# A two-layer transformer kernel: the loads of the modulation weights move from SyncE's queue to GpSimd's

## The chip, the cores and the metric

The kernel runs on one core of one Trainium2 chip. The time is the device time of one execution in microseconds (us): the median of three runs. An engine executes its own instruction list in order; an instruction whose inputs or whose target buffer are not there yet holds everything behind it on the same engine. A DMA is started by an instruction in such a list: SyncE (SP) computes nothing here and only starts DMAs, GpSimd (POOL) computes and starts DMAs.

## The reference

One call computes two blocks on a sequence of 512 tokens with 1024 features, in float32. Block one normalises `x`, projects it with `w_in`, runs a sparse attention of eight heads (compressed, selected and windowed keys) and a stick-breaking attention of eight heads, mixes both and adds an MLP. Block two runs an mLSTM and a block-sparse attention and then a mixture of 32 experts. Both blocks are modulated: a vector `mod = silu(c) @ ada_w + ada_b` of 6 x 1024 numbers is cut into shift, scale and gate for the first half of a block (columns 0, 1, 2) and for its second half (3, 4, 5), and used as

```
u = rms_norm(h, norm1_g) * (1 + scale1) + shift1
h = h + gate1 * mixed
u2 = rms_norm(h, norm2_g) * (1 + scale2) + shift2
h = h + gate2 * ff
```

The second block does the same with `c_2` and `w_ada_2`. Each of the two modulation matrices is 1024 x 6144 float32, 24 MB.

## The kernel before, in words

All large products are made on TensorE (PE) at about float32 accuracy: each weight piece is split by ScalarE (ACT) and VectorE (DVE) into two parts (`parts`, line 118), and three matmuls (`mm3`, lines 128 to 130) take the place of one. A weight piece of 1 MB is loaded by `load` (line 97) on SP's queue into one of two buffers named `raw`; a load waits until the splits of the piece before last are done.

The first two columns of the first modulation matrix are needed at once and are made on TensorE (`ada_first`, line 359, tile `araw` with 12 buffers). The other ten columns are made in the background by `ada` (line 388), off TensorE: for a column r, sixteen loads (line 399) of 128 x 512 float32, 256 KB each, go to a ring of three buffers, also named `araw`; each is multiplied by one number per row and added up. For an even k DVE does it (lines 408 and 410), for an odd k ACT multiplies in place (line 404) and POOL adds (line 406). At the end POOL adds the two sums (line 414), and TensorE adds over the partitions. Columns 2, 3, 4 of the first matrix are made during the attentions and the merge, column 5 and all six of the second matrix during the MLP. That makes 10 x 16 = 160 loads.

The instruction lists are made when the program is built. The code yields the background work in steps (`step`) after each piece of a projection; a planner then simulates the run, and puts on each engine the ready instruction that is earliest in the program, so that work of a later line may stand early in an engine's list where that engine would have been free. `self.order(a, b)` tells the planner to put a behind b: the background's multiplications are put behind the matmul of their step (`self.behind`), and the first loads of column 2 behind `self.first_loads`, the last load of `ada_first`. On the chip the lists then run in that fixed order, whatever the real durations are.

POOL's list in this part of the program also holds: copies for the attention heads (line 506), part of the softmax scaling (line 722), the second half of the split in the stick-breaking heads (line 767), stores and loads of 256 KB of the gates (lines 1094 and 985), part of the norms (lines 185 and 228), and the first weights of the compression (`compress_start`, whose last load is kept as `self.compress_loads`).

Of the kernel before, what the change touches and what calls it, by code (L numbers as in the profile page):

```python
# [72 lines left out]
class Kernel:  # L73
# [314 lines left out]
    def ada(self, which, rounds, together=False):  # L388


        nc = self.nc
        w, bname, c, mods = ((self.a["ada_w"], "ada_b", self.sc[:, 0:8], self.mods),
                             (self.a["w_ada_2"], "b_ada_2", self.sc[:, 8:16], self.mods2))[which]
        for r in rounds:
            acc = [self.apool.tile([128, 1024], F32, name=f"acc{i}", bufs=1) for i in range(2)]
            for k in range(8):
                for at in (0, 512):
                    raw = self.apool.tile([128, 512], F32, name="araw", bufs=3)
                    ins = nc.sync.dma_start(raw, w[0, k * 128:(k + 1) * 128, r * 1024 + at:r * 1024 + at + 512])
                    if which == 0 and r == 2:  # L400
                        self.order(ins, self.first_loads)
                    x = acc[k % 2][:, at:at + 512]
                    if k % 2:
                        ins = nc.scalar.activation(x if k == 1 else raw, raw, AF.Copy, scale=c[:, k:k + 1])  # L404
                        if k > 1:
                            nc.gpsimd.tensor_add(x, x, raw)  # L406
                    elif k == 0:
                        ins = nc.vector.tensor_scalar(x, raw, c[:, 0:1], None, op0=OP.mult)
                    else:
                        ins = nc.vector.scalar_tensor_tensor(x, raw, c[:, k:k + 1], x, op0=OP.mult, op1=OP.add)  # L410
                    self.order(ins, self.behind)
                if k < 7:
                    yield
            self.order(nc.gpsimd.tensor_add(acc[0], acc[0], acc[1]), self.behind)
            if together:
                if r == 0:
                    pick = self.free[:, 2048:2059]
                    nc.vector.tensor_scalar(pick, self.one[:, 0:1].to_broadcast([128, 11]), 0.0, None, op0=OP.mult)
                    nc.vector.tensor_copy(pick[:, 5:6], self.one[:, 0:1])
                    rows = self.ps("O", 1), self.ps("T", 2)  # L420
                parts = [self.free[:, i:i + 1024] for i in (0, 1024)]
                self.order(nc.scalar.activation(parts[0], acc[0], AF.Copy), self.behind)
                nc.gpsimd.tensor_sub(parts[1], acc[0], parts[0])
                for i in range(2):
                    for x in range(2):
                        nc.tensor.matmul(rows[i][:6], pick[:, 5 - r:11 - r], parts[x][:, i * 512:i * 512 + 512],
                                         start=(r + x == 0), stop=(r + x == 6), skip_group_check=True)
                yield
                continue
            ps = self.ps("T", 2)  # L430
            for j in range(8):
                nc.tensor.matmul(ps[:, 2 * j:2 * j + 2], acc[0][:, j * 128:(j + 1) * 128], self.one[:, 0:2],
                                 start=True, stop=True, skip_group_check=True)
            nc.vector.tensor_add(mods[:, r * 8:(r + 1) * 8], ps[:, :16].rearrange("p (j x) -> p j x", x=2)[:, :, 0],
                                 self.col(bname)[:, r * 8:(r + 1) * 8])
            yield
        if together:
            x = self.apool.tile([128, 1024], F32, name="acc1", bufs=1)
            for i in range(2):
                nc.scalar.activation(x[:6, i * 512:i * 512 + 512], rows[i][:6], AF.Copy)  # L440
            ps = self.ps("T", 2)
            for j in range(8):
                nc.tensor.transpose(ps[:, 6 * j:6 * j + 6], x[:6, j * 128:(j + 1) * 128], self.ident[:6, :6])
            nc.vector.tensor_add(mods.rearrange("p (r j) -> p r j", r=6),
                                 ps[:, :48].rearrange("p (j r) -> p r j", j=8),
                                 self.col(bname).rearrange("p (r j) -> p r j", r=6))
            yield
# [1659 lines left out]
```

## Time and profile before

| | |
|---|---|
| median of 3 runs | 1790.49 us (1790.27 to 1791.97) |
| profiled execution | 1795.8 us, of which the span from first to last instruction is 1794.0 us |
| TensorE (PE) busy | 1722.5 us, 96% of the span |
| VectorE (DVE) busy | 1385.7 us, 77% |
| ScalarE (ACT) busy | 1149.6 us, 64% |
| GpSimd (POOL) busy | 461.2 us, 26% |
| mean granted TensorE clock | 0.988 of full speed |
| issues of `araw` on SP, line 399 | 64 of `ada_w` and 96 of `w_ada_2`, 256 KB each, from 27.4 to 824.3 us |

The page gives shares over the whole span, and the change bears on the stretch from 27 to 830 us alone. In a row of waits, "A <- B" reads: instructions of A stood idle until B ended; a bracket such as "[2.29 <-DVE kT L171]" at the end of a row of the timeline is the idle time of that engine just before the row, and what ended it.

### The profile page before, as it was taken

To read this page: it belongs to the slowest core of one execution; us is meant where nothing else is said; L and a number is where in the kernel's file an instruction comes from. 1 tells how busy PE (TensorE), PEld (TensorE's weight loads), DVE (VectorE), ACT (ScalarE), POOL (GpSimd) and SP (SyncE) were. 2 spreads that over 40 slices of the span, in tenths; PEclk is the share of its full clock that TensorE was granted. 3 is DMA by queue.
4 is the path that set the end of the run, shared out by engine and by line. 5 is a ranking of instruction groups with operands and counts; after the bars stand their busy time and mean duration, and the time that the engine had idled before them with its cause. 6 is when DMAs were issued, how large, how long until landed. Compare 5 with 4: busy or idle time off the path is not lost. (4 is left out here: it accounts for less than half of the span.)

```text
span 1794.0 us, 24961 instructions
## 1 busy us (share of the span) xinstructions
PE 1722.5 (96%) x8996; PEld 1414.4 (79%) x8996; DVE 1385.7 (77%) x2028; ACT 1149.6 (64%) x1814; POOL 461.2 (26%) x428
## 2 busy tenths in 40 slices
PE   6999999998999999999999999979999989999996
PEld 3878977887898888888978888757877767787874
DVE  4758788887687474747756877879999979999997
ACT  4646765764555343435555765568888868888886
POOL 2114326435032333333313300111212112121113
PEclk9999999998999999999999999989999999999998
DMA  9543204217446655554432224669999999999954
GB/s 344 172 130 106 78 30 160 87 60 245 149 152 210 201 184 192 187 188 159 141 95 71 71 67 165 233 203 366 366 360 366 327 323 381 374 367 365 371 209 168
DMA packets 234912, 377.71 MB, mean 211 GB/s; under 512 B 11817, under 2 KB 102565, under 8 KB 234784
## 3 DMA queue, kind: packets, MB, share of 16 engines
q1 hardware_dynamic: 223904, 348.22, 56.5%
q0 software_dynamic: 10880, 27.85, 5.2%
q8 instruction: 72, 1.18, 0.3%
q14 instruction: 56, 0.46, 0.1%
HBM read 366.64 MB, written 20.73 MB: 216 GB/s over the span
## 5 line engine op out<-in xcount | busy, mean ns | idle before, releaser
L118 ACT ACTIVATE w<-raw 128x1024 fp32r<-128x1024 f32 (+2 forms) x350 | 353.8, 1017 | 298.4 <-PE G L129 230.5
L118 DVE TENSOR_TENSOR w<-raw,w 128x1024 fp32r<-128x1024 f32 (+2 forms) x350 | 421.9, 1225 | 115.6 <-ACT w L118 113.8
L128 PE MATMUL G<-u,w 128*128 128x512 f32 (+1 forms) x688 | 265.5, 387 | 3.2 <-DVE mo L1090 1.3
L129 PE MATMUL G<-u,w 128*128 128x512 f32 (+1 forms) x688 | 264.4, 385 | 2.0 <-DVE u L922 1.1
L130 PE MATMUL G<-u,w 128*128 128x512 f32 (+1 forms) x688 | 264.7, 386 | 0.6 <-DVE w L118 0.6
L129 PE MATMUL S<-w,x 128*128 128x512 f32 x504 | 200.9, 399 | 0.8 <-DVE w L118 0.8
L128 PE MATMUL S<-w,x 128*128 128x512 f32 x504 | 196.2, 395 | 5.4 <-PEq L1933 5.2
L130 PE MATMUL S<-w,x 128*128 128x512 f32 x504 | 198.2, 393 | 0.0
L118 DVE TENSOR_TENSOR w<-rawa,w 128x1024 fp32r<-128x1024 f32 x122 | 151.2, 1271 | 15.4 <-ACT w L118 15.3
L128 PEld LDWEIGHTS G<-u,w 128*128 128x128 f32 x688 | 129.8, 189 | 30.4 <-issue 2.8
L129 PEld LDWEIGHTS G<-u,w 128*128 128x128 f32 x688 | 129.8, 189 | 27.9 <-DVE u L922 1.6
L118 ACT ACTIVATE w<-rawa 128x1024 fp32r<-128x1024 f32 x122 | 127.7, 1059 | 36.7 <-PE S L130 23.0
L130 PEld LDWEIGHTS G<-u,w 128*128 128x128 f32 x688 | 129.9, 189 | 26.3 <-DVE w L118 1.8
L406 POOL TENSOR_TENSOR acc<-acc,araw 128x512 f32<-128x512 f32 x60 | 87.6, 1479 | 236.8 <-ACT araw L404 236.6
L128 PEld LDWEIGHTS S<-w,x 128*128 128x128 f32 x504 | 95.7, 190 | 27.2 <-issue 5.7
L129 PE MATMUL G<-hid,w 128*128 128x512 f32 (+1 forms) x320 | 111.1, 347 | 1.2 <-DVE hid L1131 1.2
L129 PEld LDWEIGHTS S<-w,x 128*128 128x128 f32 x504 | 95.7, 190 | 20.3 <-DVE w L118 1.1
L130 PE MATMUL G<-hid,w 128*128 128x512 f32 (+1 forms) x320 | 111.3, 348 | 0.0
L130 PEld LDWEIGHTS S<-w,x 128*128 128x128 f32 x504 | 95.7, 190 | 19.7 <-DVE x L1773 0.3
L128 PE MATMUL G<-hid,w 128*128 128x512 f32 (+1 forms) x320 | 110.8, 347 | 0.0
L129 PE MATMUL G<-w,hh 128*128 128x512 f32 x248 | 100.7, 406 | 2.3 <-DVE w L118 0.9
L1737 POOL TENSOR_TENSOR x<-xg,x 128x512 fp32r<-128x512 f32 x30 | 44.9, 1498 | 218.9 <-ACT x L1736 218.9
(652 smaller groups left out, 4028.8 us busy)
## 6 DMA issues: line engine op xcount, KB each, us to landing
raw<-in_mlp_w_dram SPq DMA_DIRECT2D x36, 1024.0 KB, 5.5
raw<-in_w_in_dram SPq DMA_DIRECT2D x33, 1024.0 KB, 5.4
raw<-in_w_expert_up_dram SPq DMA_DIRECT2D x28, 1024.0 KB, 9.6
raw<-in_w_expert_gate_dram SPq DMA_DIRECT2D x27, 1024.0 KB, 9.2
raw<-in_w_expert_down_dram SPq DMA_DIRECT2D x27, 1024.0 KB, 8.1
araw<-in_w_ada_dram SPq DMA_DIRECT2D x96, 256.0 KB, 3.7
rawa<-in_w_expert_gate_dram SPq DMA_DIRECT2D x21, 1024.0 KB, 9.5
rawa<-in_w_expert_up_dram SPq DMA_DIRECT2D x20, 1024.0 KB, 8.5
```

What stands on the lines that cost most here:

```text
L118: ins = nc.scalar.activation(r[0], v, AF.Copy), nc.vector.tensor_sub(r[1], v, r[0])
L128: first = nc.tensor.matmul(ps, lhs[0], rhs[0], start=start, stop=False)
L129: nc.tensor.matmul(ps, lhs[0], rhs[1], start=False, stop=False)
L130: self.behind = nc.tensor.matmul(ps, lhs[1], rhs[0], start=False, stop=stop)
L406: nc.gpsimd.tensor_add(x, x, raw)
L1737: nc.gpsimd.tensor_sub(x[1][:, s], y[:, s], x[0][:, s])
```

## The change

The instruction that starts the 160 loads of `ada` is issued by GpSimd in place of SyncE. The first loads of column 2 are ordered behind the last load of `compress_start`, which is on GpSimd's queue, and no longer behind the last load of `ada_first`, which is on SyncE's. The ring of three buffers, the sizes, the consumers and their order behind the matmuls are the same.

```diff
@@ -396,9 +396,9 @@
             for k in range(8):
                 for at in (0, 512):
                     raw = self.apool.tile([128, 512], F32, name="araw", bufs=3)
-                    ins = nc.sync.dma_start(raw, w[0, k * 128:(k + 1) * 128, r * 1024 + at:r * 1024 + at + 512])
+                    ins = nc.gpsimd.dma_start(raw, w[0, k * 128:(k + 1) * 128, r * 1024 + at:r * 1024 + at + 512])
                     if which == 0 and r == 2:
-                        self.order(ins, self.first_loads)
+                        self.order(ins, self.compress_loads)
                     x = acc[k % 2][:, at:at + 512]
                     if k % 2:
                         ins = nc.scalar.activation(x if k == 1 else raw, raw, AF.Copy, scale=c[:, k:k + 1])
```

## Rows read from the trace of the kernel before

**Rows 1.** Busy time by stretch: length, then each engine's, PEclk, DMA share, GB/s.
```profile
100.00:200.00 100.00, 99.84 (x568) 83.96 (x567) 78.55 (x198) 65.17 (x144) 30.54 (x41) 1.00 0.37 114
280.00:320.00 40.00, 37.25 (x181) 29.44 (x180) 35.51 (x38) 23.12 (x41) 26.27 (x19) 0.99 0.53 171
405.00:440.00 35.00, 30.26 (x119) 23.36 (x119) 24.09 (x39) 18.02 (x30) 19.17 (x25) 0.85 0.72 230
540.00:820.00 280.00, 280.00 (x1255) 230.41 (x1254) 171.06 (x187) 124.76 (x169) 87.34 (x51) 1.00 0.59 192
```

**Rows 2.** Waits from 400 to 445 us: total us, times, longest.
```profile
DVE acc L410 <- DMA araw<-in_ada_w_dram: 7.0, 4, 3.1
ACT araw L404 <- DMA araw<-in_ada_w_dram: 4.5, 3, 3.8
```

**Rows 3.** TensorE's timeline, the longest of five idle times from 412 to 430 us.
```profile
427.76 0.79 PE L129 MATMUL G<-kT,w 128*128 128x512 f32 x1 [2.29 <-DVE kT L171]
```

**Rows 4.** VectorE's timeline in the same stretch: start us, us, work, idle before.
```profile
413.64 1.02 DVE L410 SCALAR_TENSOR_TENSOR acc<-araw,sc,acc 128x512 f32<-128x512 f32 x1 [3.09 <-DMA araw<-in_ada_w_dram]
414.58 0.62 DVE L783 CAST P<-e 128x512 fp32r<-128x512 f32 x2
...
426.35 0.75 DVE L410 SCALAR_TENSOR_TENSOR acc<-araw,sc,acc 128x512 f32<-128x512 f32 x1 [2.49 <-DMA araw<-in_ada_w_dram]
427.02 0.69 DVE L171 TENSOR_TENSOR kT<-sq,qT 128x512 fp32r<-128x512 f32 x1
```

**Rows 5.** Busy time in the two stretches behind the longest idle times.
```profile
417.20:420.40 3.20, 3.16 (x8) 2.51 (x9) 1.94 (x3) 0.18 (x1) 0.00 (x0) 0.50 0.64 243
...
427.70:434.20 6.50, 6.44 (x15) 4.64 (x16) 5.19 (x9) 3.95 (x7) 2.98 (x6) 0.50 0.64 197
```

**Rows 6.** Line 399 by stretch (from 563; 275 to 317; 405 to 440): ns min/median/max, starts.
```profile
L399 SPq DMA_DIRECT2D araw<-in_w_ada_dram x96: 327/328/1147, 563.6 to 824.3; - x96
...
L399 SPq DMA_DIRECT2D araw<-in_ada_w_dram x16: 327/328/383, 275.2 to 316.0; - x16
...
L399 SPq DMA_DIRECT2D araw<-in_ada_w_dram x14: 327/360/588, 406.3 to 438.6; - x14
```

**Rows 7.** A held weight load: its issue on SP, and the split that freed its buffer.
```profile
578.57 0.39 SPq L97 DMA_DIRECT2D raw<-in_mlp_w_dram  x1
...
575.80 1.22 DVE L118 TENSOR_TENSOR w<-raw,w 128x1024 fp32r<-128x1024 f32 x1
```

**Rows 8.** The start: SP's timeline, then the stretch by engine.
```profile
27.37 3.04 SPq L399 DMA_DIRECT2D araw<-in_ada_w_dram  x3
...
20.00:40.00 20.00, 17.64 (x141) 8.64 (x140) 9.21 (x17) 8.20 (x12) 1.93 (x3) 1.00 1.05 383
```

**Rows 9.** ScalarE's waits from 540 to 840 us.
```profile
ACT w L118 <- PE G L129: 138.7, 47, 4.4
ACT acc L404 <- DMA araw<-in_w_ada_dram: 20.4, 8, 6.0
```

**Rows 10.** Issues of loads of 256 KB on POOL, line 985, and their landing.
```profile
L985 POOL DMA_DIRECT2D sg<-md x13: 539/544/573, 414.8 to 451.9; - x13
...
DMA to landing us min/median/max: 3.2/6.2/7.2
```

**Rows 11.** Line 767 on POOL: durations, and who waited for it in the run.
```profile
L767 POOL TENSOR_TENSOR s<-e,s x24: 726/1376/2252, 299.3 to 405.0; 128x512 fp32r<-128x512 f32 x16, 128x256 fp32r<-128x256 f32 x8
...
PE S L770: 0.2, 1
```

**Rows 12.** POOL's timeline: a split, loads of the gates.
```profile
391.39 0.73 POOL L767 TENSOR_TENSOR s<-e,s 128x256 fp32r<-128x256 f32 x1 [4.29 <-DVE s L766]
...
414.85 1.09 POOL L985 DMA_DIRECT2D sg<-md  x2 [0.75 <-DMA md<-mo]
...
431.21 0.56 POOL L985 DMA_DIRECT2D sg<-md  x1 [6.17 <-DVE sg L992]
```

**Rows 13.** SP's longest wait for a buffer from 400 to 445 us, ending at 406.30.
```profile
SPq L399 <- DVE acc L408: 22.7, 1, 22.7
```

## The prediction

> **What bounds the kernel now.** I began with the page: TensorE is busy for 96% of the span, so a change off TensorE can win only where TensorE stands idle, and lose only where it makes TensorE wait. The busy time by stretch says where that is while the background loads run [rows 1]. From 540 to 820 us, where most of them lie, TensorE is busy 280.00 of 280.00 us; from 100 to 200 us it is 99.84 of 100. Two stretches have gaps: 280 to 320 us (2.75 idle) and 405 to 440 us (35.00 - 30.26 = 4.74 idle, granted clock 0.85).
>
> Then I asked who waits for whom in the second of these. VectorE waited 7.0 us and ScalarE 4.5 us for the loads in question [rows 2]. The reader should see in the timelines how this reaches TensorE: an addition of the background (line 410) stands in VectorE's list ahead of a cast and of a split that TensorE needs; it waits 3.09 and 2.49 us for its load [rows 4], and TensorE is idle until the cast, and until the split [rows 3]. Both times the granted clock then is 0.50, which is 1.2 GHz in place of 2.4, for 3.20 and 6.50 us [rows 5]. Half of 9.70 us, 4.85 us, is lost to that. So late loads cost this stretch up to 4.74 + 4.85 = 9.6 us, and the question is whether GpSimd brings them sooner.
>
> **The change part by part.** *What SP gets back.* 160 issues at 0.328 us are 52.5 us of SP [rows 6]. SP computes nothing, so this counts only where a weight load stood behind one of them. The widest case that I found: the split that frees the buffer ends at 577.02, the weight load is issued at 578.57, 1.55 us late [rows 7]; the TensorE of that stretch has no gap. I take 0; a gain of 1.5 us is the other end.
>
> A page's rule can stand beside that. The rows above show issue time that nobody waited for. The Trainium skill, "DMA: Bandwidth & Descriptors", section "Issuing engines are not separate DMA queues", says that starting DMAs from several engines saves only the sequencer's time to start them. This case's rows agree so far as the 52.5 us go; by the rule the change can win no bandwidth.
>
> *The start.* The three first loads leave SP at 27.37 us and would go out behind GpSimd's compression loads instead. They are 0.77 MB, at 383 GB/s 2.0 us of transfer, in a crowded stretch [rows 8]. They stand behind the loads that TensorE waits for there, so moving them frees nothing that is late: 0, and at best -2.0.
>
> *What GpSimd takes on.* A load of the same size takes 0.539 to 0.573 us of GpSimd [rows 10], so 160 of them take about 88 us, and each needs a place in its list. That makes the trip through the ring of three buffers longer: the release of a buffer, the issue, the landing, the use. The issue grows by 0.55 - 0.33 = 0.22 us, and the issue may have to stand behind an instruction of GpSimd.
>
> *The MLP, 540 to 820 us.* 96 loads and most of column 5. GpSimd is busy 87 of 280 us, and 53 to 59 more fit. ScalarE stands 138.7 us waiting for TensorE, and has already swallowed a wait for such a load of 6.0 us without a gap on TensorE [rows 1, 9]. The cover is TensorE's own queue of ready work; it would be gone if a load came more than about 6 us later than now. I take 0; the bad end is one such wait, +6. The stretch from 100 to 200 us has the same cover: 0, bad end +2.75, the gap that 280 to 320 shows.
>
> *The stick-breaking heads, 275 to 317 us.* 16 loads [rows 6], 16 x 0.55 = 8.8 us more on GpSimd, which is busy 26.27 of 40 us there [rows 1]: 35 of 40. Its other work here is the split of line 767, median 1.376 us, for which TensorE waited 0.2 us in all [rows 11]. 16 loads through 3 buffers are 5.3 trips; in 66% of the cases GpSimd is busy when the buffer comes free, and half an instruction is 0.7 us, so a trip is 0.22 + 0.66 x 0.7 = 0.68 us longer and the round 3.6 us. What share reaches TensorE I take from 405 to 440 us: 4.74 idle for 11.5 us waited [rows 1, 2], 41%. That is +1.5 us. Ends: 0 (all hidden) and +8.8 (all of GpSimd's new work on the path).
>
> *The merge, 405 to 440 us.* 14 loads, 4.7 trips [rows 6]; GpSimd is busy 19.17 of 35 us, 55% [rows 1], so a trip is 0.22 + 0.55 x 0.7 = 0.6 us longer, 2.8 us together, of which 41% are 1.1 us of idle time; the clock took as much again as the idle time there (4.85 to 4.74): +2.3 us. There is also a new neighbour: on GpSimd the loads share the list with loads of the gates, one of which held the list 6.17 us until 431.21 [rows 12]. The buffer that line 410 frees at 427.10 [rows 4] would be refilled 4.1 us later if its load stood behind that one; 41% of it is 1.7, with the clock 3.4; I give this even odds, +1.7. Ends of the stretch: -9.6 (both waits gone) and +9.6 (as much again).
>
> Sum: 0 + 0 + 0 + 1.5 + 2.3 + 1.7 = +5.5 us. The profiled execution takes 1795.8 us, 5.3 above the median of 1790.49, and would take 1801.3; against the median that is 1796.0 us.
>
> **The rivals.** *Hidden anyway.* Almost nobody waits for GpSimd today: 0.2 us of TensorE's for line 767 [rows 11], and the 0.22 us per trip could vanish in the covers named. For it: full TensorE in most of the stretch. Against it: the two stretches without cover. Time: 1790.5, give or take 3.
>
> *Faster: the two waits fall out of the order.* The planner places the background's additions where it expects their loads. If, with the loads on another engine, it puts the additions of line 410 behind the cast and the split that TensorE needs, VectorE's two waits hurt nobody, and the 9.6 us come back: 1780.9, and with one of the two, about 1785. It decides at a single place: whether line 410 stands ahead of line 783 and line 171 [rows 4]. For it: the waits show that today's order rests on loads expected sooner than they come. Against it: on GpSimd they come later still, and the planner may go wrong elsewhere.
>
> *Much slower: a load that blocks GpSimd.* SP could afford to wait 22.7 us for a buffer until 406.30 [rows 13]. On GpSimd such a wait holds what follows. Were it placed ahead of the split at 391.39 [rows 12], that would come 14.9 us late: up to 1805.4. Against it: the planner sees both on one engine and would place the load after the split.
>
> *Slower by the port.* VectorE and GpSimd might get in each other's way. But the casts at 414.58, beside two loads issued by GpSimd at 414.85, took 0.62 for two, and the thirteen issues of line 985 never took over 0.573 us [rows 4, 10, 12]. So issuing does not seem to suffer. If it did, with each of the 10 trips 0.88 us longer (the difference of line 767's longest and median [rows 11]), 41% of it with the clock would be about 7 us: 1803. The Trainium skill, "SBUF — State Buffer", the box "The DVE blocks DMA trap (SWDGE)", states that mechanism: while VectorE runs in a two-port mode GpSimd cannot write its descriptors. It gives about 0.62 us alone and 3.1 us beside a copy; by that each trip would be an estimated 2.5 us longer, and the kernel some 20 us slower. The thirteen rows don't bear it out.
>
> **How the numbers follow.** The forecast (+2 to +10) 0.38; hidden 0.25; faster 0.26; blocked 0.07; port 0.04. A change within 0.2%, 3.6 us, can't be told from none here. Nearly all of the forecast's chance and the last two are slower by more than that: 0.47, the rest of the forecast (0.02) going to the same, 0.27; faster 0.26. The forecast's own range is 1792 to 1801. To leave out no more than 2 in 10 the range has to reach to the faster case's full price and past the blocked one's: 1781 to 1807.
>
> **What would show it.** Right: line 399 on POOL's queue at about 0.55 us each; TensorE still full from 540 to 820; in the merge and the stick-breaking heads more waits for `araw` on VectorE and ScalarE than 11.5 us, more idle TensorE, and a clock of 0.50 behind it. Wrong: no wait of line 410 ahead of a cast (the faster case), TensorE's idle time as before (hidden), or a new gap outside the two stretches, above all one that is ended by GpSimd.

## The result, and the profile after

The changed kernel takes 1804.61 us (median of four runs, 1801.05 to 1810.33), the kernel before 1791.23: a ratio of 1.0076, 95% interval 1.0055 to 1.0098, so slower by 13.4 us. A second measurement, beside the experiments, gave 1801.81 us and 1.0055 (1.0040 to 1.0071), 10.7 us. The forecast was slower by 5.5 us.

The program falls into five parts, whose ends can be read from the lines that begin and end them: line 706 is the last product of the sparse attention's heads, line 1128 the first result of the MLP, line 1230 the end of its half of the block, line 2011 the last store, which GpSimd issues. First the kernel before, then the changed one (a row holds count, duration in ns as min/median/max, and the first and last start in us).

```profile
L706 PE MATMUL O<-C,vsc x16: 587/640/692, 150.2 to 267.4; 32*128 32x512 f32 x16
...
L1128 ACT ACTIVATE r<-G x30: 572/578/599, 540.7 to 833.1; 128x512 f32<-128x512 f32 x30
...
L1230 DVE SCALAR_TENSOR_TENSOR h<-G,mods,h x16: 743/748/752, 1091.1 to 1154.9; 128x512 f32<-128x512 f32 x16
...
L2103 POOLq DRAIN  x3: 50/115/5038, 1788.2 to 1793.8; - x3
```

```profile
L706 PE MATMUL O<-C,vsc x16: 587/640/692, 151.2 to 272.0; 32*128 32x512 f32 x16
...
L1128 ACT ACTIVATE r<-G x30: 576/578/601, 544.4 to 845.4; 128x512 f32<-128x512 f32 x30
...
L1230 DVE SCALAR_TENSOR_TENSOR h<-G,mods,h x16: 743/749/752, 1103.4 to 1167.2; 128x512 f32<-128x512 f32 x16
...
L2103 POOLq DRAIN  x3: 50/262/8312, 1799.0 to 1808.3; - x3
```

The attention's end is 4.6 us later (272.0 to 267.4). From there to the MLP's start nothing is lost: 272.4 us after, 273.3 before. The MLP, from the first line 1128 to the last line 1230, takes 622.8 in place of 614.2, so 8.6 more. The experts behind it gain 1.5 in this pair of profiles. The rest is behind the last instruction: GpSimd's closing DRAIN takes 8.312 in place of 5.038 us, and from the start of line 2011 to the end of the span it is 9.4 us in place of 5.6.

The stretches of [rows 1] again, in the changed kernel (length, busy time of PE, PEld, DVE, ACT, POOL, then PEclk, DMA share, GB/s):

```profile
100.00:200.00 100.00, 98.68 (x545) 82.74 (x544) 79.66 (x191) 61.26 (x134) 40.69 (x57) 0.98 0.36 111
280.00:320.00 40.00, 39.06 (x186) 32.02 (x187) 36.02 (x42) 23.93 (x43) 30.30 (x32) 0.96 0.53 171
405.00:440.00 35.00, 31.25 (x142) 24.95 (x141) 29.46 (x47) 18.92 (x34) 22.99 (x33) 0.90 0.58 185
540.00:820.00 280.00, 275.53 (x1232) 227.16 (x1231) 165.60 (x179) 119.80 (x161) 136.03 (x152) 0.98 0.58 186
```

The two stretches that were full have gaps now (1.32 us from 100 to 200, 4.47 from 540 to 820), and the two that had gaps are a little fuller. VectorE's 7.0 us of waits for the loads in the merge [rows 2] have shrunk to this one row:

```profile
DVE acc L410 <- DMA araw<-in_ada_w_dram: 1.1, 1, 1.1
```

The 160 loads are on GpSimd, and their issues cost what [rows 10] said (0.539 us the shortest, 0.539 and 0.547 the medians); landing takes 3.3 us in the median:

```profile
L399 POOL DMA_DIRECT2D araw<-in_w_ada_dram x96: 539/539/582, 572.0 to 836.8; - x96
L399 POOL DMA_DIRECT2D araw<-in_ada_w_dram x64: 539/547/754, 43.1 to 568.1; - x64
...
DMA to landing us min/median/max: 2.8/3.3/9.5
```

**The gap at 580 us.** TensorE's timeline shows two idle times (the bracket at the end of a row is the idle time before it and what ended it):

```profile
578.77 0.39 PE L130 MATMUL G<-hid,w 128*128 128x512 f32 x1
581.88 3.57 PE L432 MATMUL T<-one,acc 128*128 128x2 f32 x16 [2.72 <-POOL acc L414]
587.20 0.80 PE L128 MATMUL G<-hid,w 128*128 128x512 f32 x1 [1.75 <-DVE h L1135]
```

Line 432 is the sum over the partitions that finishes column 5, the gate of the MLP. Without it the first `add` (line 1135) of the MLP's second product can't run, and that product has only two PSUM banks (`G`): when both are full, TensorE has to wait for the gate. GpSimd's timeline shows how its last addition came late, VectorE's what stood between line 432 and the `add`:

```profile
568.11 0.54 POOL L399 DMA_DIRECT2D araw<-in_ada_w_dram  x1 [1.03 <-DVE acc L410]
...
577.25 1.29 POOL L406 TENSOR_TENSOR acc<-acc,araw 128x512 f32<-128x512 f32 x1 [3.42 <-ACT araw L404]
578.49 0.56 POOL L399 DMA_DIRECT2D araw<-in_w_ada_dram  x1
579.06 2.76 POOL L414 TENSOR_TENSOR acc<-acc,acc 128x1024 f32<-128x1024 f32 x1
```

```profile
580.06 2.85 DVE L118 TENSOR_TENSOR w<-raw,w 128x1024 fp32r<-128x1024 f32 x1 [0.43 <-ACT w L118]
585.49 0.17 DVE L434 TENSOR_TENSOR mods<-T,cols 128x8 f32<-128x8 f32 x1 [2.58 <-PE T L432]
585.60 0.88 DVE L408 TENSOR_SCALAR acc<-araw,sc 128x512 f32<-128x512 f32 x2
586.40 1.40 DVE L1135 SCALAR_TENSOR_TENSOR h<-G,mods,h 128x512 f32<-128x512 f32 x2
```

After the gap the granted clock is 1.2 GHz for some ten microseconds (PEclk, third from the end, 0.51):

```profile
582.00:592.00 10.00, 8.25 (x28) 7.16 (x29) 4.59 (x8) 1.44 (x2) 3.02 (x6) 0.51 0.61 200
```

So 4.47 us of idle time and some 4 us by the clock (half of the 8.25 us of work in these ten) make the 8.6. In the profile of the second measurement (a1 below) line 432 waited 0.64 us in place of 2.72, and the MLP took 619.8, 5.6 more than before:

```profile
578.45 1.95 PE L432 MATMUL T<-one,acc 128*128 128x2 f32 x16 [0.64 <-POOL acc L414]
...
582.21 0.80 PE L128 MATMUL G<-hid,w 128*128 128x512 f32 x1 [1.81 <-DVE h L1135]
```

In the kernel before, line 432 came without a wait and ahead of the point where TensorE runs dry, and the `add` came 34.4 us after the MLP's start (575.1 - 540.7) in place of 42.0:

```profile
572.39 1.84 PE L432 MATMUL T<-one,acc 128*128 128x2 f32 x16
...
574.26 0.17 DVE L434 TENSOR_TENSOR mods<-T,cols 128x8 f32<-128x8 f32 x1 [1.99 <-PE T L432]
...
575.14 0.75 DVE L1135 SCALAR_TENSOR_TENSOR h<-G,mods,h 128x512 f32<-128x512 f32 x1
```

**The gap at 170 us.** GpSimd, VectorE and TensorE in the changed kernel:

```profile
163.23 0.55 POOL L399 DMA_DIRECT2D araw<-in_ada_w_dram  x1
163.79 2.40 POOL L414 TENSOR_TENSOR acc<-acc,acc 128x1024 f32<-128x1024 f32 x1
166.13 0.55 POOL L399 DMA_DIRECT2D araw<-in_ada_w_dram  x1
166.69 1.91 POOL L722 TENSOR_TENSOR P<-P,st 128x128 f32<-128x128 f32 x3
```

```profile
163.56 2.67 DVE L711 TENSOR_TENSOR st<-st,gates 128x4 f32<-128x4 f32 x1
...
166.92 2.77 DVE L118 TENSOR_TENSOR w<-raw,w 128x1024 fp32r<-128x1024 f32 x1
```

```profile
170.09 1.06 PE L667 MATMUL S<-kdc,QS 128*128 128x32 f32 x8 [1.32 <-DVE st L696]
```

Line 711, four numbers per partition, takes 0.17 us elsewhere and here 2.67: it ends at 166.23, when GpSimd's addition (line 414) ends. The split of line 118 takes 1.23 us elsewhere and 2.77 beside line 722. The two together hold VectorE for 4 us, and TensorE runs dry behind them. In the kernel before the same addition holds VectorE too, but there it meets a split alone (3.45 us in place of 1.23), and TensorE loses 0.16 us in all from 100 to 200 us [rows 1]:

```profile
166.87 2.38 POOL L414 TENSOR_TENSOR acc<-acc,acc 128x1024 f32<-128x1024 f32 x1
...
166.90 3.45 DVE L118 TENSOR_TENSOR w<-raw,w 128x1024 fp32r<-128x1024 f32 x1
```

The gap is not the whole price. Behind it the granted clock falls: over these 30 us it is 0.94 in the changed kernel, about 1.8 us lost. In the kernel a2 of the experiments the same gap stands, and the clock stays at 1.00 (the changed kernel first, then a2):

```profile
150.00:180.00 30.00, 28.68 (x178) 25.27 (x177) 26.19 (x69) 17.22 (x45) 14.64 (x18) 0.94 0.30 88
...
150.00:180.00 30.00, 28.68 (x183) 24.66 (x184) 26.30 (x68) 17.52 (x45) 14.97 (x20) 1.00 0.27 85
```

### The profile page after: what moved, and what is told of

Its sections match the earlier page's. It is cut to its first block, busy times and chain, and to the rows that moved or that the text cites. A ratio compares the mean times of both kernels' runs of the same rounds, so it can differ in the third digit from the quotient of the medians.

```text
span 1808.6 us, 24940 instructions
## 1 busy us (share of the span) xinstructions
PE 1728.0 (96%) x8996; PEld 1418.7 (78%) x8996; DVE 1397.5 (77%) x2028; ACT 1149.7 (64%) x1814; POOL 545.6 (30%) x588
## 5 line engine op out<-in xcount | busy, mean ns | idle before, releaser
L118 DVE TENSOR_TENSOR w<-raw,w 128x1024 fp32r<-128x1024 f32 (+2 forms) x350 | 431.2, 1251 | 112.3 <-ACT w L118 109.6
## 6 DMA issues: line engine op xcount, KB each, us to landing
raw<-in_w_expert_up_dram SPq DMA_DIRECT2D x28, 1024.0 KB, 11.5
```

Of the source, the lines that this page charges most:

```text
L118: ins = nc.scalar.activation(r[0], v, AF.Copy), nc.vector.tensor_sub(r[1], v, r[0])
```

## The experiments

Every kernel was profiled once and timed. The table gives the parts by the lines named above, in us: the last start of line 706; from there to the first line 1128; from there to the last line 1230; from there to line 2011; from there to the end of the span.

| kernel | loads on GpSimd | to 706 | to 1128 | to 1230 | to 2011 | end | median | ratio to before (95%) |
|---|---|---|---|---|---|---|---|---|
| before | 0 | 267.4 | 273.3 | 614.2 | 633.5 | 5.6 | | |
| changed | 160 | 272.0 | 272.4 | 622.8 | 632.0 | 9.4 | 1804.61 | 1.0076 (1.0055, 1.0098) |
| changed, again | 160 | 271.7 | 271.3 | 619.8 | 630.3 | 9.4 | 1801.81 | 1.0055 (1.0040, 1.0071) |
| e1 second matrix | 96 | 267.7 | 270.4 | 614.0 | 631.3 | 5.4 | 1790.12 | 0.9997 (0.9988, 1.0006) |
| e2 columns 2 to 4 | 48 | 271.3 | 271.4 | 613.6 | 631.7 | 7.9 | 1797.18 | 1.0034 (1.0021, 1.0046) |
| e3 column 5 | 16 | 267.8 | 273.3 | 618.9 | 630.6 | 6.0 | 1799.66 | 1.0052 (1.0039, 1.0066) |
| e4 all but column 5 | 144 | 272.0 | 270.0 | 613.9 | 629.7 | 7.6 | 1797.59 | 1.0040 (1.0026, 1.0054) |
| e6 order alone | 0 | 267.4 | 271.1 | 614.2 | 629.1 | 5.6 | 1790.06 | 0.9994 (0.9984, 1.0004) |
| e8 64 of the second | 64 | 267.1 | 272.0 | 613.9 | 629.8 | 8.5 | 1793.98 | 1.0021 (1.0010, 1.0031) |
| h1 mix | 96 | 266.9 | 272.6 | 613.9 | 629.7 | 5.4 | 1792.45 | 1.0010 (1.0001, 1.0019) |
| a2 gate taken from column 2 | 160 | 269.4 | 271.6 | 614.1 | | | | |
| a3 line 414 on VectorE | 160 | 268.3 | 275.0 | 618.3 | 631.0 | 9.4 | 1804.86 | 1.0082 (1.0065, 1.0098) |
| a4 line 406 of column 5 on VectorE | 160 | 271.2 | 271.8 | 619.3 | 632.1 | 9.3 | 1801.58 | 1.0055 (1.0040, 1.0071) |
| a5 four PSUM banks | 160 | 271.9 | 269.8 | 613.6 | 630.9 | 9.3 | 1798.12 | 1.0035 (1.0023, 1.0048) |

The columns "to 1128" and "to 2011" scatter by some 1.5 us between kernels whose lists are the same there (e1 and before differ by nothing ahead of the MLP, and by 2.9 us in "to 1128"), so single differences of that size mean nothing. The first and the third column fall into two groups each, with 3.4 and 4.1 us between them (a2 and a3 apart in the first); the fifth goes from 5.4 to 9.4.

### Which loads cost

Theory A was that column 5's deadline makes the MLP's 8.6 us and column 2 the attention's; rival B that each load costs its share.

```diff
-                    ins = nc.sync.dma_start(raw, w[0, k * 128:(k + 1) * 128, r * 1024 + at:r * 1024 + at + 512])
+                    ins = (nc.gpsimd if which == 1 else nc.sync).dma_start(raw, w[0, k * 128:(k + 1) * 128, r * 1024 + at:r * 1024 + at + 512])
+                    ins = (nc.gpsimd if which == 0 and r < 5 else nc.sync).dma_start(raw, w[0, k * 128:(k + 1) * 128, r * 1024 + at:r * 1024 + at + 512])
+                    ins = (nc.gpsimd if which == 0 and r == 5 else nc.sync).dma_start(raw, w[0, k * 128:(k + 1) * 128, r * 1024 + at:r * 1024 + at + 512])
+                    ins = (nc.gpsimd if not (which == 0 and r == 5) else nc.sync).dma_start(raw, w[0, k * 128:(k + 1) * 128, r * 1024 + at:r * 1024 + at + 512])
```

(Against the kernel before; the lines added are those of e1, e2, e3 and e4. e2 and e4 take the new order of the first loads too.)

> Only the 96 loads of the second matrix go to GpSimd; those of columns 2 to 5 stay on SyncE. Theory A (column 5's deadline at the start of the MLP costs 8.6 us of it, the attention stage some 4): TensorE has no gap from 605 to 840 us in either trace, so these 96 loads cost nothing: 1791, within 1.5 us, apart from the wait at the very end of the program. Rival B (each load that GpSimd issues costs about the same, 13.4 us over 160): 96/160 of it, 8.0 us, 1799. Rival C (what grows is GpSimd's drain behind the last instruction, with the number of its DMAs): the drain of 5.0 us before, 8.3 us after, should be about 7 here, +2.

> Only the 48 loads of columns 2, 3 and 4 go to GpSimd, with the new order of the first loads. Theory A: the attention stage alone pays, TensorE's last line 706 about 4.6 us later than before (267.4), the MLP begins about 3.7 us later (540.7 before), and column 5, on SyncE, is in time for the first addition of its gate (575.1 before): 1794 to 1796. Rival B (equal cost per load): 48/160 of 13.4, 4.0 us, 1795; told from A by the milestones, which under B would go on falling behind past 540 us. Rival C (drain): about 6 us of drain.

> Only the 16 loads of column 5 go to GpSimd. Theory A: the MLP begins when it did before (540.7 us), but the column is finished late, behind 581 us, TensorE stands at line 432 for the last addition of GpSimd (line 414) and then runs at a granted clock of 0.50: some +8 us, 1798 to 1800. Rival B (equal cost per load): 16/160 of 13.4, 1.3 us, 1792.5.

> All loads but the 16 of column 5 go to GpSimd. Theory A: the change without the wait at line 432: only the 4 us of the attention stage and what the drain takes: 1794 to 1797. Rival B (equal cost per load): 144/160 of 13.4, 12 us, 1803. Rival D (the gap at the MLP's start comes from the change of the instruction lists in all, not from column 5's loads being on GpSimd): a gap of some 8 us of TensorE between 560 and 600 us here too, 1802.

Measured: e1 changes nothing, with 60% of the loads; e3 costs 9.2 us, with 10% of them. Rival B is out. The first column splits the kernels by who issues column 2 (266.9 to 267.8 on SyncE, 271.2 to 272.0 on GpSimd, a3 apart, and a2, whose 269.4 has the gap without the lower clock), the third by who issues column 5 (613.6 to 614.2, against 618.3 to 622.8, a2 and a5 apart). Rival D is out by e4, whose lists are rearranged too, and which has no gap (TensorE is busy for 40.00 of the 40 us from 560 to 600). e2 and e4 came out 1.2 and 0.6 us above the upper ends of theory A's times, in which the drain had no full share. e3's time is in theory A's range, but the gap has another shape than theory A said, and than in the changed kernel:

```profile
575.99 1.95 PE L432 MATMUL T<-one,acc 128*128 128x2 f32 x16
...
580.75 0.80 PE L128 MATMUL G<-hid,w 128*128 128x512 f32 x1 [2.81 <-DVE h L1135]
```

Line 432 does not wait, it is over before 581 us, and the gap still comes. That it is late data alone was thereby in doubt.

### Why column 5 costs

In a2, a4 and a5 (in this order) the changed kernel is altered:

```diff
-                    nc.vector.scalar_tensor_tensor(x, ps, mods[:, 40 + k:41 + k], x, op0=OP.mult, op1=OP.add)
+                    nc.vector.scalar_tensor_tensor(x, ps, mods[:, 16 + k:17 + k], x, op0=OP.mult, op1=OP.add)
-                            nc.gpsimd.tensor_add(x, x, raw)
+                            (nc.vector if which == 0 and r == 5 else nc.gpsimd).tensor_add(x, x, raw)
-                    self.project(hid, "mlp_w2", 0, D, add, f * 8)
+                    self.project(hid, "mlp_w2", 0, D, add, f * 8, banks=() if f else (("G", 2), ("G", 2), ("S", 3), ("S", 3)))
```

> The changed kernel, but the MLP's result is multiplied by column 2 in place of column 5, so that column 5 is made and loaded by GpSimd as before but nothing in the MLP waits for it. Theory A (the deadline): the gap of TensorE at 580 us is gone, and the time is that of the kernel that left column 5 on SyncE, 1797, within 1.5. Rival D (the loads slow the MLP's start in another way, by the DMA engines or by GpSimd's list): the gap stays, 1803 to 1805.

With the deadline gone the MLP takes 614.1 us, and TensorE has no idle row from 540 to 605 us, though column 5 is loaded by GpSimd and finished at 582.1. The times behind line 1230 can't be compared, nor the total (1941.83 us), against what I had expected: with the other gate the numbers that the experts get are others, and behind line 1230 TensorE has 2937 matmuls in place of 2760. That the tokens go to other experts is the likely reason; no run shows it.

> The changed kernel, with the six additions of column 5 that GpSimd makes (line 406) on VectorE, so that GpSimd's list holds loads and the last addition alone there. Theory I (column 5 is late because loads and additions stand in each other's way in GpSimd's list): the column is done before the first addition of its gate, no gap of TensorE at 580 us, 614 us from the MLP's first line 1128 to the last line 1230 in place of 620 to 623: 1796 to 1798. Rival J (each load simply takes longer from GpSimd): still late, 618 to 620, 1800 to 1802.

Theory I fell. The column's data are indeed ready earlier: GpSimd's last addition ends at 575.12, 32.1 us after the MLP's start, in place of 37.4 in the changed kernel (581.82 - 544.4). It doesn't help:

```profile
572.73 2.39 POOL L414 TENSOR_TENSOR acc<-acc,acc 128x1024 f32<-128x1024 f32 x1 [4.66 <-DVE acc L406]
```

```profile
577.67 1.84 PE L432 MATMUL T<-one,acc 128*128 128x2 f32 x16
582.49 0.80 PE L128 MATMUL G<-hid,w 128*128 128x512 f32 x1 [2.98 <-DVE h L1135]
```

Line 432 could have run at 575.1 and runs at 577.67, with no wait: it is where it stands in TensorE's list. Counted in the lists as built, the second product's matmuls ahead of line 432 are 35 in the kernel before, 41 in e4, and 48 in e3, a4 and the changed kernel; two banks take 2 x 24 = 48. So with column 5 on GpSimd the planner puts its last step behind everything that can be done without it, and the road from there to the gate (the sum, line 434, two of line 408 in VectorE's list, the `add`; in e3 and a4 a split of 1.23 us ahead of line 434 too) is uncovered, and in a4 earlier data don't change that. In the kernel before 13 matmuls of 0.23 us, 3.0 us, were left to cover it. Why the planner does so no run tells; that it expects the column later is my reading. No run moves line 432 alone either: that its place is the cause rests on a4, on e4 with its 41, and on a5.

> The changed kernel, with the MLP's first four products of the second weight (mlp_w2) in two PSUM banks of G and two of S, which are free there, in place of two of G alone. Theory L (the place in TensorE's list: with column 5's loads on GpSimd the column sum, line 432, stands behind all 48 matmuls that two banks can take, in the kernel before behind 35 of them, so that nothing is left to cover the wait for the gate; here it stands behind 68 of 96): no gap of TensorE between 560 and 600 us, 614 us from the MLP's first line 1128 to the last line 1230, 1796 to 1798, what is left being the attention stage (4) and the drain (3). Rival J (column 5's data come too late from GpSimd whatever the list): the gap stays, 618 to 623 us, 1801 to 1804.

Theory L held. Line 432 comes at 580.84, 39.1 us after the MLP's start and no earlier than in the changed kernel (37.5), the `add` 41.9 after it as there (583.6 - 541.7), and TensorE is full at the full clock, because two more banks hold the next products:

```profile
580.84 1.84 PE L432 MATMUL T<-one,acc 128*128 128x2 f32 x16
```

```profile
560.00:600.00 40.00, 40.00 (x186) 33.40 (x185) 22.59 (x25) 15.17 (x20) 19.32 (x24) 1.00 0.58 185
```

### Why the attention costs

e6 is the kernel before with the new order alone, a3 the changed kernel with one addition moved:

```diff
-                        self.order(ins, self.first_loads)
+                        self.order(ins, self.compress_loads)
-            self.order(nc.gpsimd.tensor_add(acc[0], acc[0], acc[1]), self.behind)
+            self.order(nc.vector.tensor_add(acc[0], acc[0], acc[1]), self.behind)
```

> All loads stay on SyncE; only the order is changed: the first loads of column 2 go behind the compression's loads, as in the change. Theory G (the attention stage is slower because the first loads come later and the lists are put in another order): TensorE's last line 706 at 271 to 272 us as in the changed kernel (267 to 268 before), 1794. Theory H (it is slower because GpSimd issues the loads of column 2 between its own work): 267 to 268, 1790.5. GpSimd's drain about 5 us under both.

The last line 706 starts at 267.4 and the time is that of before: theory H, the new order of the first loads costs nothing; that GpSimd issues column 2 does.

> The changed kernel with the last addition of each column (line 414, ten of them, 2.4 to 3.3 us each) on VectorE (about 1.2 us each). Theory E (in the attention stage that addition on GpSimd holds VectorE up: line 711 took 2.67 us beside it in place of 0.17, line 118 2.77 in place of 1.23): TensorE's gap of 1.32 us at 170 us goes, line 706 ends 2 to 3 us earlier than in the changed kernel, and column 5 is ready 2 us earlier: 1799 to 1801. Rival F (the lists are only in another order, the slow instructions are no cause): line 706 ends at 272 as before, and only column 5 gains: 1802 to 1804.

```profile
162.92 1.19 DVE L414 TENSOR_TENSOR acc<-acc,acc 128x1024 f32<-128x1024 f32 x1
164.11 1.22 DVE L118 TENSOR_TENSOR w<-raw,w 128x1024 fp32r<-128x1024 f32 x1
```

In this stage theory E came out: with the addition on VectorE neither line 711 nor the split is held (at most 0.17 and 1.23 us), TensorE has no gap from 100 to 230 us, and the last line 706 starts at 268.3, 3.4 to 3.7 us earlier. The forecast of the total did not: 275.0 us to line 1128 give it back in this profile, and a3 is no faster (1804.86 against 1801.81 of a1). Since the edit also rearranges the lists, it shows that the attention's cost can be had back up to line 706, and it agrees with the held instructions as the cause; it doesn't exclude that another order would have done the same.

### What the tail is

The loads on GpSimd in e8 and h1, against line 399 of the kernel before; a1 is the changed kernel again:

```diff
+                    ins = (nc.gpsimd if which == 1 and r < 4 else nc.sync).dma_start(raw, w[0, k * 128:(k + 1) * 128, r * 1024 + at:r * 1024 + at + 512])
+                    ins = (nc.gpsimd if r < 4 and (which == 1 or r == 3) or which == 0 and r == 4 else nc.sync).dma_start(raw, w[0, k * 128:(k + 1) * 128, r * 1024 + at:r * 1024 + at + 512])
```

> The changed kernel as it is, measured again. Both theories: 1801 to 1806, 13 above before. Theory C1 (GpSimd's drain behind the last instruction goes by how many DMAs it has issued, in a cycle of 96 of these loads: 5.04, 5.45, 7.33, 4.79, 7.00 and 8.31 us were seen with 0, 16, 48, 96, 144 and 160 more): 8.0 to 8.6 us again. Theory C2 (the drain's length is chance): anything from 4.8 to 8.3.

> Only the first 64 loads of the second matrix (four of its six columns) go to GpSimd. Up to GpSimd's drain both theories expect the time of before. Theory C1 (drain by the number of DMAs, 64 being where 160 stands in a cycle of 96): a drain of about 8.3 us, 1794. Theory C3 (a long drain comes with the loads of columns 2 to 4): 5 us, 1790.5.

> A mix: columns 2 and 5 on SyncE with the old order, columns 3 and 4 and the first 64 loads of the second matrix on GpSimd, 96 loads in all. Theory A with C1 (only column 2 and column 5 cost, and the drain goes by the number of loads in a cycle of 96): the heads and the merge take what they took in the changed kernel, some 1 us less than before, and the drain is about 5 us: 1789 to 1791. Rival K (columns 3 and 4 cost what the prediction said, 5.5): 1795 to 1797. Rival B (equal cost per load): 96/160 of 12, 7 us, 1798.

The changed kernel's drain came out at 8.312 us again (a1), so it isn't chance. e8, without one load of columns 2 to 4, has a long one, and h1, with 32 of them, has a short one, both as their number says; here e1, e8 and h1 in this order:

```profile
L2103 POOLq DRAIN  x3: 50/115/4785, 1783.2 to 1788.5; - x3
```

```profile
L2103 POOLq DRAIN  x3: 50/263/7400, 1782.6 to 1791.0; - x3
```

```profile
L2103 POOLq DRAIN  x3: 50/115/4788, 1782.9 to 1788.2; - x3
```

With 0, 16, 48 and 64 more loads on GpSimd the drain takes 5.0, 5.4, 7.3 and 7.4 us, with 96 it is back at 4.8, and 144 and 160 give 7.0 and 8.3. Rival C of e1 and e2, a drain that only grows with the number, missed both (4.8 for about 7, 7.3 for about 6). Rival C3 is out, and C1 held but for e8's 7.4, for which 8.3 was forecast. e8's total is 2.9 us up, nearly what its tail is (8.5 - 5.6). What is counted, and whether 96 is exactly its cycle, no run here tells.

h1 was the mix to which the runs pointed, without the three costs. It takes 1792.45 us, 1.5 above the upper end of theory A's time, and 1.0010 of the time before (1.0001 to 1.0019), so 1.3 us are left that I can't place; rivals K and B are out. e1 and e6 take 0.9997 and 0.9994: the costs can be avoided nearly or wholly, but there was nothing to be won, and no kernel here beats the one before.

## Why the prediction came out as it did

The sign and the wide range of 1781 to 1807 us held; the forecast's own range of 1792 to 1801 and the sum of +5.5 did not, and none of its terms is where the time went. That the sign came out is luck: every part for which a cost was forecast cost nothing. Of the prediction's own signs of being right the issues of 0.55 us were seen, but TensorE is not full from 540 to 820 us, and the waits for `araw` in the merge, which were to grow beyond 11.5 us, fell to 1.1. A sign of being wrong was seen, a new gap that GpSimd ends (2.72 us at 580).

- **The relief of SP, and the start: 0 and 0.** Right. e1 takes 96 issues off SyncE and e6 moves the first loads, and neither changes the time. The rival "hidden anyway" is true of these 96.
- **GpSimd's issues at 0.55 us, and the port rival.** Right: 0.539 to 0.754 us, though VectorE was busy beside them. The Trainium skill, "SBUF — State Buffer", the box "The DVE blocks DMA trap (SWDGE)", has it that GpSimd can't write its descriptors while VectorE is in a two-port mode. No issue of the 160 is near the 3.1 us that the prediction took from this page; whether VectorE was in such a mode beside one, no run here shows. The same page, section "Who interferes with whom", has the rule that mattered: a VectorE instruction with two inputs in SBUF contends with a GpSimd instruction that reads SBUF, by a lock that is exclusive. Line 711's 2.67 us beside line 414 agree with it, as does the split's 3.45 in the kernel before. So the prediction put its rival to the issues alone, where it is not true, and left out the additions, where it is.
- **The MLP: 0, "The cover is TensorE's own queue of ready work".** This step failed, and cost 5.6 to 8.6 us. The wait of 6.0 us that ScalarE had swallowed [rows 9] was for the second matrix, whose columns nobody needs until block two; column 5 is needed 34 us after the MLP begins. The queue of ready work ends at two PSUM banks, and what stood in it ahead of line 432 was set by the planner. A look at who needs each column, and when, would have shown it: in the kernel before, the gate was finished at 574.3 us and used at 575.1.
- **100 to 200 us: 0, bad end +2.75.** Failed too: +4.3 by line 706 (mean of the six kernels with column 2 on GpSimd and nothing else altered there, 271.7, against 267.4). About 1.3 us of it are the gap and 1.8 the clock behind it; the rest I haven't placed. I asked whether a load would be late. What came instead was that the additions of the background went to other places in GpSimd's list, and held VectorE at another moment.
- **The heads and the merge: +1.5, +2.3, +1.7.** Measured together: nothing (269.8 to 272.4 us with columns 2 to 4 on GpSimd, a3 apart, and 270.4 to 273.3 with column 2 on SyncE). In the merge the rival "the two waits fall out of the order" came true: 1.1 us in place of 7.0. But 440 to 540 us have 2.5 us less of busy TensorE than before (95.87 against 98.41), so it gave nothing back in sum.
- **The end of the program:** no term at all, +3.8 us. I looked at the 30 to 830 us in which the loads run, and the sum had no place for what a queue does behind the last instruction.

Added up, with the MLP of a1 (619.8 against 614.0, the mean of the kernels with column 5 on SyncE): 4.3 + 5.8 + 3.8 = 13.9 us, against 10.7 and 13.4 measured; the other two parts scatter by 1.5 us each, and in the second measurement's profile they lie 2 and 3.2 us below those of before.

## What to carry to other kernels

When a change makes background work later, price it by who needs its result and when, column by column, not by how long the engines that make it may wait. A step with slack in its data can still be late by its place in a fixed list: look at what the engine can do without it (here 48 matmuls in two banks), and at how much of that is left behind it. Two banks that were free were worth 6 us of the MLP (619.8 to 613.6) and some 4 of the whole (1.0055 to 1.0035 of the time before, intervals that overlap), where earlier data were worth nothing (a4).

## What the runs showed of the hardware

The closing drain of GpSimd's queue changes with how many DMAs it has issued, hundreds of microseconds earlier: by 0.03 to 0.05 us for each load of 256 KB up to 64 of them (0.4 us for 16, 2.3 for 48, 2.4 for 64), and with 96 it is as short as with none. The same idle time of TensorE can cost more or less by the clock behind it: 1.32 us at 170 us were followed by a clock of 0.72 from 171 to 177 us in the changed kernel, and by 1.00 in a2. And loads landed no later in the median from GpSimd's queue than from SyncE's, which they share with the weights: 3.3 us over all 160 in the changed kernel, 3.6 before.
